# A power pooling on one core: three squares cut in two, with the root and the store of the load ahead between the parts

## The chip, the core and the metric

The kernel runs on one core of a Trainium2 chip. The metric is device time in microseconds (us), as the median of several executions. The core's engines that matter here are ScalarE (ACT), VectorE (DVE), SyncE (SP), which issues most transfers, and the 16 DMA engines that carry them. TensorE has no work, and GpSimd only writes four constants.

## The reference

Every window of four neighbours in a row is reduced to its power mean with p = 2, that is, the root of the mean of the squares:

```python
batch, channels, length = 32, 256, 4096
kernel_size = 4
...
window = np.abs(x[:, :, start:end]) ** p
result[:, :, i] = (np.mean(window, axis=-1)) ** (1.0 / p)
```

The input has 33.55 million float32 values (134.22 MB), the output a quarter of that (33.55 MB). Every output value depends on four adjacent input values alone, so the input can be cut anywhere at a multiple of four.

## The kernel before

The input is taken as one flat array and given to 128 partitions, 262,144 values each. It is worked through in 20 loads: 19 of 13,184 values per partition and a last one of 11,648. Three tiles of SBUF hold the loads in turn (load i goes to tile i mod 3), so load i + 3 can be issued only once the sums of load i have been read out of its tile.

Each load goes through four steps. ACT squares it in place (`square`, L88). DVE adds the values of a window two by two into the first half of the tile (`pairs`, L94), and adds those pairs into one value for each window (`fours`, L98). ACT takes the root with a scale of 1/4 (`root`, L101). The result is a quarter of a load, 3,296 values per partition.

The results of four loads make a block, and a block is stored with one transfer of the same size as a load (6,592 KB). Loads 0 to 3, 4 to 7, 8 to 11 and 12 to 15 are blocks; they all use one tile of results, `ot`, whose four quarters belong to the four loads. So the sums of the next block may overwrite a quarter only after the store of the block before has read it. To put this off, the sums of loads 4, 8, 12 and 16 go to a tile in PSUM (`st`), and their roots go from there to `ot` later. The sums of loads 5, 9 and 13 are the first that have to wait for the store. The results of loads 16 to 19 are kept in a tile of the loads that is free by then (`xt`), and are stored in two transfers.

The order of work on each engine is that of the program, written by hand (`manual_schedule`). SP issues all the loads (L82), each behind the sums of three loads earlier, and the last three stores. Stores 0, 1 and 2 are issued by ACT, on a DMA queue of its own (q10 in the profile; SP's is q1), right behind the root that completes them (L85). In a round of the main loop, ACT takes first the roots that stand in `ahead`, then the square of the load, then the roots that stand in `behind`:

```python
ahead = {4: (3,), 8: (7,), 12: (11,)}
behind = {3: [(0, 1, 2)], 7: [(5, 6), (4,)], 11: [(9, 10), (8,)], 14: [(12,)], 15: [(13, 14)], 16: [(15,)]}
```

So around load 4 ACT does: square of load 3, the roots of loads 0, 1 and 2 as one instruction, the root of load 3 as soon as DVE has its sum, the issue of store 0, and the square of load 4. Around loads 8 and 12 it is the same with the blocks after (there the roots of the block's first three loads are two instructions).

`implied(later, earlier)` tells the scheduler that no wait has to be made between two instructions, because other waits already put them in order. The last two loads, 18 and 19, have a part of their squares on DVE (L151), and their own order.

Of the kernel before, what the change touches and what calls it, by code (L numbers as in the profile page):

```python
# [1 line left out]

# [4 lines left out]


@with_exitstack
def kernel(  # L10
    ctx: ExitStack,
    tc: tile.TileContext,
    x: bass.AP,
    p: float,
    kernel_size: int,
    out: bass.AP,
):

    nc = tc.nc

    assert float(p) == 2.0, "kernel specialized for p == 2"
    k = int(kernel_size)  # L30
    assert k == 4, "kernel specialized for kernel_size == 4"

    P = nc.NUM_PARTITIONS
    fp32 = mybir.dt.float32
    Act = mybir.ActivationFunctionType
    add = mybir.AluOpType.add
    xf = x.rearrange("b c l -> (b c l)")
    of = out.rearrange("b c l -> (b c l)")
    total = xf.shape[0] // P

    W = 13184
    R = W // k
    X_SLOTS = 3
    LAST = total - 19 * W
    widths = [W] * 19 + [LAST]
    n = len(widths)
    assert 0 < LAST <= W and LAST % 16 == 0


    blocks = [[0, 1, 2, 3], [4, 5, 6, 7], [8, 9, 10, 11], [12, 13, 14, 15], [18, 16, 17], [19]]  # L50
    block_of = {i: b for b, group in enumerate(blocks) for i in group}
    block_width = [sum(widths[i] for i in group) for group in blocks]

    x_pool = ctx.enter_context(tc.tile_pool(name="x_pool", bufs=1))
    o_pool = ctx.enter_context(tc.tile_pool(name="o_pool", bufs=1))
    s_pool = ctx.enter_context(tc.tile_pool(name="s_pool", bufs=1, space=bass.MemoryType.PSUM))
    x_tiles = [x_pool.tile([P, W], fp32, name=f"xt{j}") for j in range(X_SLOTS)]
    o_tile = o_pool.tile([P, 4 * R], fp32, name="ot")
    first = o_pool.tile([P, 1], fp32, name="first")
    s_tile = s_pool.tile([P, 4096], fp32, name="st")  # L60
    ctx.enter_context(tc.manual_schedule())

    def rows(flat, b, div):
        at = sum(block_width[:b]) * P // div
        return flat[at:at + block_width[b] * P // div].rearrange("(p w) -> p w", p=P)


    free = x_tiles[17 % X_SLOTS]
    place = {i: o_tile[:, i % 4 * R:(i % 4 + 1) * R] for i in range(16)}
    place[18] = free[:, R:2 * R]  # L70
    place[19] = free[:, 0:LAST // k]
    place[16] = free[:, 2 * R:3 * R]
    place[17] = free[:, 3 * R:4 * R]
    held = [o_tile[:, :]] * 4 + [free[:, R:4 * R], place[19]]

    xs, loads, stores, sums = {}, {}, {}, {}

    def load(i):
        b = block_of[i]
        at = sum(widths[j] for j in blocks[b][:blocks[b].index(i)])  # L80
        xs[i] = x_tiles[i % X_SLOTS][:, 0:widths[i]]
        loads[i] = nc.sync.dma_start(out=xs[i], in_=rows(xf, b, 1)[:, at:at + widths[i]])  # L82

    def store(b, queue):
        stores[b] = queue.dma_start(out=rows(of, b, k), in_=held[b])  # L85

    def square(v):
        return nc.scalar.activation(out=v, in_=v, func=Act.Square)  # L88

    def pairs(v):  # L90

        q = v.rearrange("p (n j) -> p n j", j=k)
        h = v[:, 0:v.shape[1] // 2].rearrange("p (n j) -> p n j", j=2)
        return nc.vector.tensor_tensor(out=h, in0=q[:, :, 0:2], in1=q[:, :, 2:4], op=add)  # L94

    def fours(o, v):
        h = v[:, 0:v.shape[1] // 2].rearrange("p (n j) -> p n j", j=2)
        return nc.vector.tensor_tensor(out=o, in0=h[:, :, 0], in1=h[:, :, 1], op=add)  # L98

    def root(o, s):  # L100
        return nc.scalar.activation(out=o, in_=s, func=Act.Sqrt, scale=1.0 / k)  # L101

    summed = {i: s_tile[:, 0:R] if i in (4, 8, 12, 16) else place[i] for i in range(n)}

    def roots(*group):
        if len(group) == 1:
            root(place[group[0]], summed[group[0]])
        else:
            v = o_tile[:, group[0] % 4 * R:(group[-1] % 4 + 1) * R]
            r = root(v, v)  # L110
            if group[0] in (5, 9):

                implied(r, stores[block_of[group[0]] - 1])
        if group[-1] in (3, 7, 11):
            store(block_of[group[-1]], nc.scalar)

    def implied(later, earlier):

        tc.declare_no_dep(later.ins, earlier.ins, reason="implied by the other waits")

    for i in range(X_SLOTS):
        load(i)


    ahead = {4: (3,), 8: (7,), 12: (11,)}
    behind = {3: [(0, 1, 2)], 7: [(5, 6), (4,)], 11: [(9, 10), (8,)], 14: [(12,)], 15: [(13, 14)], 16: [(15,)]}

    root(first[:, :], nc.const_aps.tensor(1.0, (P, 1), fp32))
    for i in range(17):
        if i in ahead:  # L130
            roots(*ahead[i])
        s = square(xs[i])
        if i in (3, 7, 11):

            for earlier in sums[i - X_SLOTS]:
                implied(s, earlier)
        for group in behind.get(i, []):
            roots(*group)
        sums[i] = pairs(xs[i]), fours(summed[i], xs[i])
        if i + X_SLOTS < n:  # L140
            load(i + X_SLOTS)

    store(3, nc.sync)
    square(xs[17])
    pairs(xs[17])
    fours(summed[17], xs[17])
    later = {18: 4608, 19: 2000}

    def shared_square(i):
        v = xs[i][:, 0:later[i]]  # L150
        nc.vector.tensor_tensor(out=v, in0=v, in1=v, op=mybir.AluOpType.mult)  # L151
        square(xs[i][:, later[i]:widths[i]])

    def shared_pairs(i):
        implied(pairs(xs[i]), loads[i])

    shared_square(18)
    roots(16)
    roots(17)
    shared_pairs(18)  # L160
    fours(summed[18], xs[18])
    shared_square(19)
    roots(18)
    store(4, nc.sync)
    shared_pairs(19)
    fours(summed[19], xs[19])
    roots(19)
    store(5, nc.sync)


# [1 line left out]
_INS = ['x', 'p', 'kernel_size']  # L172
_OUTS = [((32, 256, 1024), 'float32')]

_NUMBERS = {'p': 2.0, 'kernel_size': 4}


# [26 lines left out]
```

## Time and profile before

| What | us |
|---|---|
| Median of 3 runs | 393.9 (393.82 to 394.01) |
| The profiled execution | 393.96 |
| Its span in the profile | 392.2 |
| ACT busy | 274.4 (70%), 37 instructions |
| DVE busy | 218.2 (56%), 42 instructions |
| ACT idle until a load landed | 90.9, 13 times |
| ACT idle until the sum of load 3, 7 or 11 was there | 7.0, 3 times |
| DVE idle until ACT had squared | 144.3, 18 times |
| DVE idle until a store had landed | 17.1, 3 times |
| A full load, issue to landing (median) | 29.7 |
| A store issued by ACT, issue to landing (median) | 35.1 |

Times inside the profile are counted from the start of its span. The profiled execution takes 1.8 us more than its span; what lies outside is not traced. In the lines of the timeline, the columns are the start, the duration, the engine, the line of the kernel, the operation with its tiles and shapes, how many such instructions were merged, and in brackets how long the engine was idle before and what ended that wait. In the groups by shape, the columns after the bar are the busy time in us, the mean of one instruction in ns, and the idle time just before them. "GB/s" in the slices and stretches counts a packet where it begins, so that short stretches are uneven.

### The profile page before, as it was taken

How to read it: one execution, taken by the hardware profiler on the slowest of the kernel's cores; microseconds unless marked ns; L12 is line 12 of the kernel's file. 1: busy time of each engine (PE TensorE's matmuls, PEld its weight loads, DVE VectorE, ACT ScalarE, POOL GpSimd, SP SyncE). 2: the span in 40 equal slices, each digit the busy share in tenths (PEclk: the TensorE clock that was granted, in tenths of full speed). 3: DMA queues.
4: the chain of work that ended last, by engine and by line, in shares of the span. 5: the costliest groups of instructions: out<-in, count | busy, mean ns of one | idle time of the engine just before them, and what ended most of it. 6: DMA issues, size and time to landing. Idle time of an engine off the chain costs nothing.

```text
span 392.2 us, 176 instructions
## 1 busy us (share of the span) xinstructions
DVE 218.2 (56%) x42; ACT 274.4 (70%) x37; POOL 0.2 (0%) x4
## 2 busy tenths in 40 slices
DVE  0008477490593374905942748069418485699980
ACT  1095685979950859799509597995098999969910
POOL 0000000000000000000000000000000000000000
DMA  8999999999999999999999999999999999999997
GB/s 344 430 430 441 436 436 441 436 436 387 430 430 430 430 430 430 430 436 430 446 441 452 446 441 436 430 430 430 430 430 430 430 430 430 430 428 438 430 413 342
DMA packets 3744, 167.77 MB, mean 428 GB/s; under 512 B 416, under 2 KB 416, under 8 KB 416
## 3 DMA queue, kind: packets, MB, share of 16 engines
q1 hardware_dynamic: 3312, 147.52, 87.4%
q10 hardware_dynamic: 432, 20.25, 11.9%
HBM read 134.22 MB, written 33.55 MB: 428 GB/s over the span
## 4 chain that ended last, share of the span: by engine, by line
DMA 43%; ACT 31%; DVE 23%; issue 0%; ACTq 0%; SPq 0%; DVEq 0%
DMA xt<-in_x_dram 43%; ACT xt L88 28%; DVE xt L94 14%; DVE ot L98 5%; DVE xt L98 3%; DVE xt L151 2%; ACT ot L101 2%; ACT xt L101 1%; ACTq L85 0%; SPq L82 0%; DVEq L94 0%
## 5 line engine op out<-in xcount | busy, mean ns | idle before, releaser
L88 ACT ACTIVATE xt<-xt 128x13184 f32<-128x13184 f32 (+2 forms) x20 | 216.7, 10847 | 92.2 <-DMA xt<-in_x_dram 90.9
L94 DVE TENSOR_TENSOR xt<-xt 128x6592 f32<-128x6592 f32 (+1 forms) x20 | 139.7, 6986 | 144.6 <-ACT xt L88 144.3
L98 DVE TENSOR_TENSOR ot<-xt 128x3296 f32<-128x3296 f32 x13 | 46.7, 3592 | 17.5 <-DMA out_dram<-ot 17.1
L101 ACT ACTIVATE ot<-ot 128x3296 f32<-128x3296 f32 (+2 forms) x8 | 37.2, 4656 | 7.0 <-DVE ot L98 7.0
L101 ACT ACTIVATE xt<-xt 128x3296 f32<-128x3296 f32 (+1 forms) x3 | 8.5, 2840 | 8.8 <-DVE xt L98 8.8
L98 DVE TENSOR_TENSOR st<-xt 128x3296 f32<-128x3296 f32 x4 | 14.4, 3600 | 0.1
L98 DVE TENSOR_TENSOR xt<-xt 128x3296 f32<-128x3296 f32 (+1 forms) x3 | 10.4, 3458 | 0.1
L101 ACT ACTIVATE ot<-st 128x3296 f32<-128x3296 f32 x3 | 8.7, 2899 | 0.0
L151 DVE TENSOR_TENSOR xt<-xt 128x4608 f32<-128x4608 f32 (+1 forms) x2 | 7.2, 3593 | 0.0
L101 ACT ACTIVATE xt<-st 128x3296 f32<-128x3296 f32 x1 | 2.9, 2899 | 0.0
L101 ACT ACT_TABLE_LOAD x1 | 1.3, 1283 | 0.7 <-PEq L185 0.7
L101 ACT ACTIVATE first<-const-float32-1.0 128x1 f32<-128x1 f32 x1 | 0.2, 203 | 0.0
L185 POOL MEMSET const-bfloat16-1.0<- 128x1 bf16 x1 | 0.1, 101 | 0.0
L185 POOL MEMSET const-uint8-127<- 128x1 uint8 x1 | 0.1, 101 | 0.0
L185 POOL MEMSET const-float32-0.0<- 128x1 f32 x1 | 0.1, 98 | 0.2 <-issue 0.2
L185 POOL MEMSET const-float32-1.0<- 128x1 f32 x1 | 0.1, 98 | 0.0
## 6 DMA issues: line engine op xcount, KB each, us to landing
xt<-in_x_dram SPq DMA_DIRECT2D x19, 6592.0 KB, 29.7
out_dram<-ot ACTq DMA_DIRECT2D x3, 6592.0 KB, 35.1
out_dram<-ot SPq DMA_DIRECT2D x1, 6592.0 KB, 37.0
xt<-in_x_dram SPq DMA_DIRECT2D x1, 5824.0 KB, 21.9
out_dram<-xt SPq DMA_DIRECT2D x1, 4944.0 KB, 16.1
out_dram<-xt SPq DMA_DIRECT2D x1, 1456.0 KB, 8.2
```

Of the source, the lines that this page charges most:

```text
L88: return nc.scalar.activation(out=v, in_=v, func=Act.Square)
L94: return nc.vector.tensor_tensor(out=h, in0=q[:, :, 0:2], in1=q[:, :, 2:4], op=add)
L98: return nc.vector.tensor_tensor(out=o, in0=h[:, :, 0], in1=h[:, :, 1], op=add)
L101: return nc.scalar.activation(out=o, in_=s, func=Act.Sqrt, scale=1.0 / k)
L151: nc.vector.tensor_tensor(out=v, in0=v, in1=v, op=mybir.AluOpType.mult)
L185: nc = _bacc.Bacc("TRN2", target_bir_lowering=False, num_devices=1)
```

## The change

The squares of loads 4, 8 and 12 are cut in two along the values: 7,600 and 5,584 for load 4, 7,296 and 5,888 for loads 8 and 12. The root of load 3, 7 or 11, and with it the issue of store 0, 1 or 2, moves from in front of the square to between its parts. DVE's sums of these loads still take the whole load, behind both parts. The other added lines are calls of `implied`, which leave out waits that the new parts would otherwise bring; the first part of such a square waits for its load, and the second part waits for nothing. No other instruction of any engine changes its place. The lines of the kernel behind the change move by up to 11.

```diff
-    ahead = {4: (3,), 8: (7,), 12: (11,)}
+    ahead = {4: 7600, 8: 7296, 12: 7296}
...
         if i in ahead:
-            roots(*ahead[i])
-        s = square(xs[i])
+            halves = square(xs[i][:, 0:ahead[i]]), roots(i - 1), square(xs[i][:, ahead[i]:W])
+        else:
+            s = square(xs[i])
         if i in (3, 7, 11):
 
             for earlier in sums[i - X_SLOTS]:
                 implied(s, earlier)
+        if i in (7, 11, 15):
+            implied(s, halves[0])
+            implied(s, halves[2])
         for group in behind.get(i, []):
             roots(*group)
         sums[i] = pairs(xs[i]), fours(summed[i], xs[i])
+        if i in ahead:
+            implied(sums[i][0], loads[i])
+            implied(sums[i][1], loads[i])
         if i + X_SLOTS < n:
             load(i + X_SLOTS)
+            if i in ahead:
+                implied(loads[i + X_SLOTS], loads[i])
...
-        square(xs[i][:, later[i]:widths[i]])
+        return square(xs[i][:, later[i]:widths[i]])
...
-    shared_square(18)
+    s = shared_square(18)
+    implied(s, halves[0])
+    implied(s, halves[2])
```

## The prediction

> **What bounds the kernel now.** I read three views, in this order. First the page's slices of the span, for the transfers:
>
> ```profile
> DMA  8999999999999999999999999999999999999997
> GB/s 344 430 430 441 436 436 441 436 436 387 430 430 430 430 430 430 430 436 430 446 441 452 446 441 436 430 430 430 430 430 430 430 430 430 430 428 438 430 413 342
> ...
> HBM read 134.22 MB, written 33.55 MB: 428 GB/s over the span
> ```
>
> The 16 DMA engines are busy in every slice, and the rate hardly moves, except for slice 10 (387, from 88.2 to 98.0 us), the two ends, and 413 near the end. Then the same by stretches (columns: stretch, its length, busy us of DVE, ACT and POOL, clock, DMA share, GB/s):
>
> ```profile
> 20.00:90.00 70.00, 42.47 (x8) 54.44 (x6) 0.00 (x0) 1.00 1.00 433
> 90.00:98.00 8.00, 0.00 (x0) 7.54 (x2) 0.00 (x0) 1.00 1.02 389
> 98.00:170.00 72.00, 42.48 (x8) 49.58 (x8) 0.00 (x0) 1.00 1.00 434
> ```
>
> DMA is at 1.00 throughout; ACT and DVE have idle time in each stretch. There is one weak place, 90 to 98 us. Third, the timeline, for the loads' landings, since a square that follows a wait for its load starts as that load lands:
>
> ```profile
> 65.95 11.19 ACT L88 ACTIVATE xt<-xt 128x13184 f32<-128x13184 f32 x1 [4.40 <-DMA xt<-in_x_dram]
> ...
> 87.86 2.95 ACT L101 ACTIVATE ot<-ot 128x3296 f32<-128x3296 f32 x1 [2.38 <-DVE ot L98]
> 90.84 0.38 ACTq L85 DMA_DIRECT2D out_dram<-ot  x1
> 91.27 22.27 ACT L88 ACTIVATE xt<-xt 128x13184 f32<-128x13184 f32 x2 [0.46 <-ACT ot L101]
> ...
> 144.40 11.19 ACT L88 ACTIVATE xt<-xt 128x13184 f32<-128x13184 f32 x1 [4.39 <-DMA xt<-in_x_dram]
> ...
> 222.26 11.19 ACT L88 ACTIVATE xt<-xt 128x13184 f32<-128x13184 f32 x1 [4.39 <-DMA xt<-in_x_dram]
> ...
> 300.10 11.19 ACT L88 ACTIVATE xt<-xt 128x13184 f32<-128x13184 f32 x1 [1.58 <-DMA xt<-in_x_dram]
> ```
>
> Those are the landings of loads 3, 7, 11 and 15. Between two of them lie five whole transfers, four loads and one store of the same size: 78.45, 77.86 and 77.84 us. Five times the 15.58 us between undisturbed landings (50.36 to 65.95) is 77.9. So the second and third blocks lose nothing to the compute engines, and the first loses 0.6 us, at the dip of 90 to 98 us.
>
> The sum of the whole span: 167.77 MB are 24.85 full transfers of 6.750 MB, at 15.57 us each 387.0. Ahead of them stand 3.6 us (load 0 lands at 19.20, less 15.57), the 0.6 us of the dip, and 0.9 us behind the last landing (the last store is issued at 383.16 and lands 8.2 us later, at 391.36): 392.1 of 392.2 us. The profiled execution took 393.96, 1.76 us outside the span; the median of the runs shown is 393.9.
>
> The chain of waits reads differently, and must not be taken at its word:
>
> ```profile
> DMA 43%; ACT 31%; DVE 23%; issue 0%; ACTq 0%; SPq 0%; DVEq 0%
> ```
>
> It follows a load back to its issue, and that to the sum and square that freed the slot. But the load's packets were queued behind other transfers then: load 7 is issued at 113.21 and lands at 144.40, 31.2 us for a transfer that takes 15.6 alone.
>
> **The change part by part.** *Two squares for one, three times.* From two rows by shape:
>
> ```profile
> L88 ACT ACTIVATE xt<-xt 128x9648 f32<-128x9648 f32 x1 | 8.2, 8243 | 0.8 <-DMA xt<-in_x_dram 0.8
> L88 ACT ACTIVATE xt<-xt 128x8576 f32<-128x8576 f32 x1 | 7.4, 7352 | 4.4 <-DMA xt<-in_x_dram 4.4
> ```
>
> 1072 elements more cost 891 ns: 0.831 ns each, and some 0.22 us are fixed. A part of 7600 takes 6.54 us, 5584 takes 4.86; 7296 takes 6.29, 5888 takes 5.12. Each split costs ACT 0.22 us.
>
> *ACT in block 1.* Now root (0, 1, 2) ends at 85.48, ACT waits 2.38 us for the sum of load 3, and root 3, store 0 and square 4 follow, ending at 102.46. Load 4 landed at 81.5 (issue 56.72 + 24.8), so the first part can start at 85.5 and ends at 92.0; the sum it would have waited for is ready at 87.83. Root 3 runs to 95.0, store 0 is issued from there (90.84 before: 4.2 us later), the second part ends at 100.3. Square 4 is 2.2 us earlier: 2.38 saved less 0.22. In blocks 2 and 3 the root of load 4 or 8 ends at 163.99 and 241.85, the waits are 2.33 us, and the same sum makes the stores 4.0 us later (173.25 and 251.1) and squares 8 and 12 2.1 us earlier.
>
> *What follows the earlier square.* DVE's two sums move with it, and load 7 is issued at 111.0, not 113.21. It is worth nothing: loads 5 and 6 and store 0 are still in the queues until 128 us, and load 7's packets stand behind load 6's. The same holds for loads 11 and 15. The cover is 15 us deep.
>
> *What follows the later store.* Its queue (ACT's) holds nothing else; behind its issue on ACT stands the second part, counted above. The one that waits for it is the sum of load 5 (9, 13) on DVE, which overwrites the stored tile; DVE waits 6.4, 5.5 and 5.3 us for the stores now. Store 0 lands 36.0 us after its issue, at 126.85. If that stays, it lands at 131.0. It could take longer, as its packets now begin after load 6's: before, the first came at 94.7, 3.8 us after the issue, with load 5 still running; now 98.8, when load 5 (undisturbed landing 81.5 + 15.6 = 97.1) is through and load 6 has had one packet of 1.95 us per engine (15.58 us for eight). At equal shares load 6 then finishes first and load 7 shares the rest, some 1.6 us more: 132.6. So the sum of load 5 ends at 134.6 to 136.2 and load 8 is issued at 134.7 to 136.3, against 130.61. It is late only if the queue has run dry: load 7 lands at 144.40, of which 0.7 is the tail of landing and 1.0 the way from issue to first packet (load 0: issue 0.73, first packets from 1.7). So it must be issued by 142.7: 6.4 us of cover are left of 12.1. For load 12 it is 212.1 to 213.8 against 220.6, for load 16 289.8 to 291.5 against 298.4. DVE's next work, the pairs of load 6, waits for a square that ends at about 138, after the late sum. Nothing is late next.
>
> *What the store meets.* The 0.6 us lost at 92 to 96 us is the one cost that the change could move. No row shows its cause. It stands at the first transfer of ACT's queue; at the second and third (issues at 169.29 and 247.15) the blocks lose nothing, and load 0, the first of SP's queue, also starts slowly (3.6 us ahead of 15.57, where later landings are 15.58 apart). That speaks for a price of a queue's first use, moved 4 us and paid again. From below it could vanish: -0.6, or -1.0 by the page's slice of 387 GB/s ((433 - 387) / 433 x 9.8 us). From above, it could double, +0.6. I take 0, as the nearest rows say first use.
>
> **A rule against it.** DVE waits for all three stores, and the trace of before shows 6.4 us of cover left behind a store 4 us later. The Trainium skill, DMA: Bandwidth & Descriptors, Rules for kernel authors, says to issue a transfer early and wait late, so that its fixed cost is covered. Read as a price, three stores 4 us later would add some 12 us (an estimate: the issue times above, by that rule) and give 406. Here the stores' lateness has its cover, and the sum goes by the rows.
>
> The sum: 0 from ACT, 0 from the stores, 0 from the dip: 392.2 us of span, 393.96 with what lies outside, 393.9 as a median.
>
> **The rivals.**
> - *The dip goes* (14%): the store starts at a boundary between loads and not amid load 5. For it: the dip lies where the store's first packets meet load 5's; against: blocks 2 and 3 had the same meeting and no dip. 393.3, at the least 392.9. Most of it (10%) is within 0.2%, 0.79 us, which is about what a measurement of this kernel can tell from no change.
> - *The chain is right* (3%): ACT's saved time shortens the path, 2.2 + 2.1 + 2.1 us: 387.5. Against it stand the DMA rows.
> - *Slower, the dip at each store* (7%): the store's first packets now meet a load's first packets three times. If the dip is the price of two transfers starting within about 2 us of each other, it comes in blocks 1, 2 and 3: 1.2 to 2.0 us more, 395.5. It decides as soon as blocks 2 and 3 lose 0.4 us each (0.8 together). Against: nothing in blocks 2 and 3 now.
> - *Slower, the queue runs dry* (3%): store 0 lands 6.4 us later than I allow and load 8 misses the end of load 7. At a third of the DMA instead of a half, the store would end with load 7, and sum, issue and first packet (2.4 us of landing, 3.6, 0.1, 1.0) would leave 7.1 us empty, three times: 415. Below that it costs nothing.
> - *It does not do what it says*: the order of instructions shows three more on ACT and none moved elsewhere, and load 4 is there in time. I give it nothing.
>
> **How the numbers follow.** No change 73%, between 393.5 and 394.5 with the dip's own bounds; the dip gone 14%; the others 13%. Faster by over 0.2%: 3 and 4 of the dip's 14, 7%. Slower: 7 and 3, 10%. Same: 83%. The range, 392.9 to 394.6, holds the first two cases, 87%.
>
> **What would show it.** Right: squares 7, 11 and 15 start at 144.4, 222.3 and 300.1 within 0.3 us; square 4's second part ends near 100.3; DVE waits 6 to 8 us longer for each store (its pairs come 2 us earlier, the store 4 to 6 later), 11 to 14 us each; DMA share stays 1.00; the dip of GB/s stands near 96 to 100 us. The dip gone: square 7 at 143.8. Wrong: a DMA share under 1.00 between 143 and 150, or a square 7 after 145.

## The result, and the profile after

The changed kernel takes 410.4 us (median of six runs, 405.5 to 412.6), the kernel before 394.0 (393.8 to 394.1). The ratio is 1.032, with a 95% interval of 1.028 to 1.037; it leaves out three of the six runs, which lie over 1.5% above the fastest one. Four more runs of it, beside other runs of the kernel before, gave 410.5 and 1.042 (1.040 to 1.043). Slower by 3 to 4%, then, where no change was forecast, and with 7 us between the first six runs where the kernel before has 0.3 (0.9 between the four later ones).

The page of the profiled execution (412.42 us, span 410.6) has these slices, DMA share in tenths and GB/s:

```profile
DMA  8999999999999999999999989999989899999695
GB/s 349 462 421 411 457 447 411 416 473 406 411 401 437 452 416 416 478 421 406 426 452 354 421 354 447 360 421 467 411 344 478 329 421 390 401 419 424 283 434 215
```

Before, the rate stood between 428 and 452 GB/s over nearly the whole span; now it falls to 354, 344, 329 and 283, and some slices have idle DMA engines. The stretches (start to end, length, busy us of DVE, ACT and POOL, clock, DMA share, GB/s) show where it begins:

```profile
20.00:90.00 70.00, 42.47 (x8) 56.80 (x6) 0.00 (x0) 1.00 1.00 433
90.00:98.00 8.00, 0.00 (x0) 7.55 (x3) 0.00 (x0) 1.00 1.10 461
98.00:135.00 37.00, 19.15 (x4) 14.71 (x3) 0.00 (x0) 1.00 0.98 410
135.00:170.00 35.00, 22.64 (x5) 30.61 (x5) 0.00 (x0) 1.00 1.00 434
```

Up to store 0 the two kernels are alike. While the store shares the DMA engines with load 6 (98 to 135 us) they are nearly as busy as before, 0.98 for 1.00, but move only 410 GB/s, where the kernel before moved 434 from 98 to 170 us. Alone again, the loads run at 434. The timeline has the landings:

```profile
65.77 11.19 ACT L88 ACTIVATE xt<-xt 128x13184 f32<-128x13184 f32 x1 [4.41 <-DMA xt<-in_x_dram]
...
94.59 0.38 ACTq L85 DMA_DIRECT2D out_dram<-ot  x1
...
133.24 11.19 ACT L88 ACTIVATE xt<-xt 128x13184 f32<-128x13184 f32 x1 [22.29 <-DMA xt<-in_x_dram]
133.50 3.59 DVE L98 TENSOR_TENSOR ot<-xt 128x3296 f32<-128x3296 f32 x1 [15.49 <-DMA out_dram<-ot]
...
148.82 11.19 ACT L88 ACTIVATE xt<-xt 128x13184 f32<-128x13184 f32 x1 [4.39 <-DMA xt<-in_x_dram]
...
232.99 11.19 ACT L88 ACTIVATE xt<-xt 128x13184 f32<-128x13184 f32 x1 [4.77 <-DMA xt<-in_x_dram]
...
316.37 11.19 ACT L88 ACTIVATE xt<-xt 128x13184 f32<-128x13184 f32 x1 [1.56 <-DMA xt<-in_x_dram]
```

Between the landings of loads 3, 7, 11 and 15 lie 83.05, 84.17 and 83.38 us, against 78.45, 77.86 and 77.84: 4.6, 6.3 and 5.5 us lost, 16.4 of the 18.4 by which the span grew. All three blocks lose, and about equally. The profile of the four later runs (span 408.5) has 82.77, 82.55 and 83.21 us between the same landings, so it shows the same. Load 6 lands at 133.24 (128.8 before), store 0 at 133.4.

### The profile page after: what moved, and what is told of

The parts are those of the page before. It is cut to its first block, busy times and chain, and to the rows that moved or that the text cites. A ratio compares the mean times of both kernels' runs of the same rounds, so it can differ in the third digit from the quotient of the medians.

```text
span 410.6 us, 179 instructions
## 1 busy us (share of the span) xinstructions
DVE 218.2 (53%) x42; ACT 274.3 (67%) x40; POOL 0.2 (0%) x4
## 4 chain that ended last, share of the span: by engine, by line
DMA 47%; ACT 33%; DVE 17%; issue 0%; ACTq 0%; SPq 0%; DVEq 0%
DMA xt<-in_x_dram 47%; ACT xt L88 27%; DVE xt L94 10%; ACT ot L101 5%; DVE ot L98 3%; DVE xt L98 3%; DVE xt L160 2%; ACT xt L101 1%; ACTq L85 0%; SPq L82 0%; DVEq L94 0%
## 5 line engine op out<-in xcount | busy, mean ns | idle before, releaser
L88 ACT ACTIVATE xt<-xt 128x13184 f32<-128x13184 f32 (+6 forms) x23 | 217.2, 9457 | 117.7 <-DMA xt<-in_x_dram 116.4
## 6 DMA issues: line engine op xcount, KB each, us to landing
out_dram<-xt SPq DMA_DIRECT2D x1, 4944.0 KB, 16.2
```

## The experiments

The first question was which part of the change does it: the cut square (three more instructions, loads 7, 11 and 15 issued 2 us earlier), or the store that comes 4 us later.

**A cut as short as ACT's wait.** The split alone, with the stores at their old places:

```diff
-    ahead = {4: 7600, 8: 7296, 12: 7296}
+    ahead = {4: 2600, 8: 2600, 12: 2600}
```

> The three squares stay cut in two, but the first parts are 2600 values long, 2.4 us, just as long as ACT waited in the kernel before. So the stores are issued when the kernel before issues them (90.8, 169.3, 247.2 us). If the later store is the cause, 394.0 within 0.3. If the cut itself is (more instructions, other waits, load 7 issued 2 us earlier), 405 or more.

394.1 (ratio 0.9998, 0.9984 to 1.0012), with store 0 issued at 90.7. The cut costs nothing, and gains nothing.

**The store later, nothing cut.**

```diff
 # against the kernel before
         if i in ahead:
+            for _ in range(8):
+                nc.scalar.activation(out=s_tile[:, R:4096], in_=place[i - 4][:, 0:4096 - R], func=Act.Square)
             roots(*ahead[i])
```

> Squares whole as in the kernel before, but ACT does eight small squares of results into unused PSUM (about 6.3 us, of no use to the result) ahead of the root of load 3, 7 or 11, so that the stores are issued about 4 us later than before, as in the changed kernel, and squares 4, 8 and 12 end 4 us later than before. If the later store is the cause: 403 to 412, like the changed kernel. If the cut is: 394 to 395.

396.3 (1.0056, 1.0033 to 1.0080), with store 0 issued at 95.1. Slower with no cut, but far from the changed kernel, and between the two forecasts: if the store is the cause, half a microsecond of difference in its issue matters more than the forecast allowed.

**The change for load 4 alone** (loads 8 and 12 keep root and store in front of the whole square).

> The change for load 4 alone; loads 8 and 12 as in the kernel before. If each late store costs for itself: a third of the loss, 398 to 400. If the DMA engines fall out of step once and stay so: nearly the whole, 404 or more. If the loss needs what adds up over three blocks: 394 to 395.

400.7 (1.0165, 1.0151 to 1.0179): some 40% of the loss. Its one late store costs 4.3 us before load 7 lands (82.77 us from load 3's landing to load 7's, against 78.45). The blocks whose stores are where they were lose another 1.0 and 0.5, so most of a late store's cost falls in its own block, and some behind it.

**The store later still, behind the whole square.**

```diff
 # against the kernel before
+        s = square(xs[i])
         if i in ahead:
             roots(*ahead[i])
-        s = square(xs[i])
```

> Squares whole, the root and the store behind them, so the stores are issued about 9 us later than in the kernel before, 5 later than in the changed one. If what counts is how late the store lands for the sums of load 5, 9 and 13, and so the next loads: slower than the changed kernel, 415 to 425. If what counts is that the store's first packets meet the first packets of a load: these meet load 6, 10 or 14 in its middle, and the time is 394 to 400.

394.2 (1.0000, 0.9986 to 1.0015). This run refuted lateness by itself as the cause. Its timeline:

```profile
99.33 0.38 ACTq L85 DMA_DIRECT2D out_dram<-ot  x1
...
134.51 3.59 DVE L98 TENSOR_TENSOR ot<-xt 128x3296 f32<-128x3296 f32 x1 [16.51 <-DMA out_dram<-ot]
```

The store is issued 8.5 us later than before and DVE waits until 134.5 for it, later than in the changed kernel, and it costs nothing. DVE's wait has the cover that the prediction gave it. So what counts is not how late the store is; where it meets the loads is the next candidate. Load 5's last packets end near 96 in the changed kernel.

**The store by SP, on the loads' queue** (the changed kernel with `store(block_of[group[-1]], nc.sync)`).

> The changed kernel with its cuts, but stores 0 to 2 are issued by SP, on the queue of the loads: each store stands whole between load 6 (10, 14) and the next, and no store shares the DMA engines with a load. If the loss comes from a load and a store sharing them, after a start near a load's end: 393.0 to 394.2; and if the 0.6 us dip of the kernel before was the first use of ACT's queue, it is gone too, 393.2 to 393.5. If the loss is in the cut squares or in the late store for DVE: 400 or more.

394.6 (1.0014, 1.0005 to 1.0023). Same cuts, same roots, but the store goes whole between load 6 and load 7, and the loss is gone but for half a microsecond (the forecast was 394.2 at the most). The dip is not gone: it stands in this run's twelfth slice (386 GB/s, 108 to 118 us), where the first store now begins.

```profile
GB/s 343 429 429 429 435 451 451 440 440 435 429 386 440 451 435 429 435 429 435 429 429 429 429 429 435 429 429 429 429 445 435 435 440 451 440 391 474 429 398 284
```

**Other lengths of the first part**: 5400, 9200 and 11,200 for load 4, each 304 less for loads 8 and 12.

> The changed kernel with first parts of 5400, 5096 and 5096 values, so that the stores are issued about 1.8 us earlier, 92.8 for the first (kernel before 90.8: 394; changed kernel 94.6: 405 and more). If a start of the store near the end of load 5 (about 96.5) is what costs, its packets begin at some 96 and it is as slow as the changed kernel, 400 or more. If the cost grows with the lateness of the store: 397 to 401.

> First parts of 9200, 8896 and 8896 values: stores issued about 1.3 us later than in the changed kernel, the first at 96.0, its packets from about 99.5, two packets behind the end of load 5. If only the meeting with the load's end costs: under 399. If it is the step between the DMA engines, which any start can upset: anything from 394 to 410, with several us between its runs.

> First parts of 11200, 10896 and 10896 values: stores issued about 3 us later than in the changed kernel, the first at 97.6, some 4 us behind the end of load 5 with its first packets. By the meeting with the load's end: 394 to 395, as with the store behind the whole square (99.3: 394.2). By lateness: over 405.

409.1 (1.0375, 1.0358 to 1.0393), 396.7 (1.0067, 1.0051 to 1.0084) and 394.05 (1.0003, 0.9994 to 1.0012).

**The middle of this row without a cut** (five of the small squares instead of eight), and **the load's end moved instead of the store**:

> Squares whole, five small squares into unused PSUM (4.3 us, no use to the result) ahead of the roots of loads 3, 7 and 11: the stores are issued at about 92.6 and 2 us later than before in the other blocks, as with first parts of 5400 (409), and squares 4, 8 and 12 end 2 us later than before. If the time of the store decides and the cut has no part in it: 403 to 411. If the cut or the earlier loads are needed for the loss: 394 to 397.

```diff
 # against the kernel before; the places in the results' tile follow
-    widths = [W] * 19 + [LAST]
+    widths = [W] * 5 + [LAST] + [W] * 14
```

> The kernel before, with no cut and no later store, but load 5 has 11,648 values per partition and load 19 has 13,184 (they change places in size), so load 5 ends 1.8 us earlier, near 94.4 instead of 96.2, while store 0 is still issued at 90.8: the same 3.6 us from issue to the load's end as with first parts of 5400. Blocks 2 and 3 are as before. If the distance from the store's issue to the load's end is the cause: 399 to 402, as with one late store. If it is the cut or the lateness: 394 to 395.

409.0 (1.0375, 1.0359 to 1.0390) and 403.8 (1.0215, 1.0154 to 1.0276). The second is the kernel before, its store at 90.7, and it loses about 10 us (5 in one of its four runs), more than the 5 to 8 forecast, as soon as load 5 ends 1.8 us earlier: 5.4 of them before load 7 lands (82.1 us from load 3's landing to load 7's, against 78.45 less the 1.8 that the shorter load saves), and 2 in each of the two blocks after, where the store comes no later. With the runs before, in the order of store 0's issue:

| Store 0 issued (us) | Kernel | Time (us) |
|---|---|---|
| 90.7 | first part 2600 | 394.1 |
| 90.8 | before | 394.0 |
| 92.6 | five fillers, no cut | 409.0 |
| 92.8 | first part 5400 | 409.1 |
| 94.6 | changed | 410.4 |
| 95.1 | eight fillers, no cut | 396.3 |
| 96.0 | first part 9200 | 396.7 |
| 97.5 | first part 11,200 | 394.05 |
| 99.3 | behind the square | 394.2 |

Between 90.8 and 97.5 us lies a window that is bad, whoever fills the time before it, and on both sides of it the time is that of before.

**Why the window.** The trace has a record of every DMA packet. A load and a store of full width are 128 packets each, one for each partition's row, eight on each of the 16 engines. Each packet begins where its engine's last one ended, so the records can be put back into 16 lanes (the numbering of the lanes is mine, and behind idle time the lanes are less sure, so I count block 1 alone). Two lanes of the changed kernel from 94 to 122 us; L is a load's packet, S a store's, with its us, and the first one listed is the last of load 5:

```
lane  1: L1.95 L1.95 L1.96 S2.01 L2.09 S1.95 L1.95 S1.95 L1.95 S1.95 L1.95 S1.95 L1.95 S1.95
lane 11: L1.95 L2.14 S1.95 L2.25 S2.44 L1.95 S2.66 L1.95 S2.72 L1.95 S2.66 L1.95 S2.41 L2.29
```

Once load and store alternate, a packet takes 1.95 us on nearly all lanes, but on three of them the store's mostly take 2.3 to 2.7. On those three the packets of 90 to 134 us take 4.1 to 5.4 us more in all than at 1.95 each, on the other 13 lanes 0.2 to 1.8. A load has landed when its last lane has, so three lanes hold up all, and 4.6 us is what the block lost. What sets lane 11 apart is the order: on lane 1 two packets of load 6 went ahead of the store, on lane 11 one. From then on they alternate, so on lane 11 the store's first row directly follows load 6's first row, its second the second, and so on. Over block 1 of 15 profiles (all but the store by SP and the half packets), by how many rows the load is ahead of the store's packet:

| Rows the load is ahead | Store packets | Mean us | Share over 2.05 us |
|---|---|---|---|
| -2 | 78 | 1.947 | 0% |
| -1 | 360 | 1.947 | 0% |
| 0 | 81 | 1.968 | 4% |
| 1 | 516 | 2.187 | 52% |
| 2 | 520 | 1.948 | 0% |
| 3 and 4 | 354 | 1.952 | 1% |

(At 0 the load's next packet is the one of the same row, and takes 2.1 to 2.3 us in the mean, by how the lanes are joined. In the table that moves the counts by up to a dozen, and the mean of 2.187 to 2.182. About half of the packets one row behind are not slow; what decides that stays open.) And by kernel: store packets one row behind the load number 0 in the kernel before and with 2600, 92 of 128 with 5400, 82 with five fillers, 75 with the narrow load, 29 and 37 in two profiles of the changed kernel, 44 in the change for load 4 alone, and 0 with 11,200 and behind the square; the 16 each with 9200 and eight fillers are the last packet of every lane, behind another store packet.

That is a reading of records, found after the fact: the order goes with the time. It makes two sharp forecasts: put one more packet ahead of the store on its queue, and the changed kernel (one or two rows behind the load) must recover, and the kernel before (level or ahead) must become slow.

```diff
 # against the changed kernel, first parts 430 shorter, and against the kernel before
+            b = block_of[group[-1]]
+            nc.scalar.dma_start(out=extra[:, b * 128:(b + 1) * 128], in_=o_tile[0:16, 3 * R:3 * R + 128])
             store(b, nc.scalar)
```

> The changed kernel with a small copy of 16 partitions (one packet for each DMA engine, from the results to an unused tile) on ACT's queue just ahead of each store; the first parts are 430 values shorter, so that the stores are still issued at 94.6 and at their places in blocks 2 and 3. The load gets ahead of the store by one more packet. If the slow packets are those where load and store are on the same partition's row: 394 to 397. If a start near the end of a load is what costs: 403 to 412.

> The kernel before, uncut, with the same small copy ahead of each store (the store's issue moves by 0.35 us, to 91.2). There the store is ahead of the load or level with it; one packet back brings engines to the same row. If the same row is the cause: 397 to 410. If the distance to the load's end is: 394 to 395.5, for 0.35 us is a fifth of the way to 92.8.

394.7 (1.0018, 1.0009 to 1.0027) and 410.3 (1.0405, 1.0389 to 1.0421). The issues of the copy and the store took a little longer than I had counted, so store 0 is issued at 94.9 in the first and 91.3 in the second; the second is 0.4 us from the kernel before and 16 us slower. In it, all the store's packets that could be placed in block 1 (125 of 128) are one row behind the load; in the first, none are. The copy also moves the store's issue by 0.3 to 0.4 us, but that shift alone is not what changed the order: with the store later still, at 92.8 (first part 5400), fewer packets, 92, are one row behind, and the load's lead of two to four rows in the first (54 packets at three, 70 at four) is more than the two to three rows with the store at 97.5. One stretch, 98 to 134 us, first of the recovered kernel, then of the spoilt one:

```profile
98.00:134.00 36.00, 17.65 (x3) 22.87 (x3) 0.00 (x0) 1.00 1.01 425
```

```profile
98.00:134.00 36.00, 17.65 (x3) 16.30 (x2) 0.00 (x0) 1.00 0.99 376
```

The DMA share is the same, 1.01 and 0.99; the packets take longer, and 376 GB/s are moved for 425.

**Half packets** (the changed kernel with every load and store in two transfers of half the width).

> The changed kernel, but every load and every store is issued as two transfers of half the width, so that the DMA engines alternate between load and store in packets of 26 KB instead of 52.7. If engines that fall out of step by part of a packet are the cause, half the packet is half the loss or less: 394 to 401. If the start of the store at the load's end costs whatever the packets are: 405 to 412.

396.3 (1.0053, 1.0038 to 1.0068). It agrees, but settles nothing: with twice as many packets the number of rows by which a load is ahead is another, too.

**The changed kernel again, beside those runs.**

> The changed kernel once more, on the same chip as these runs, for its profile beside theirs: 405 to 413, with more spread between its runs than the kernel before has.

410.5. On three of its lanes in block 1 the store is one row behind the load from the first packet on, and 37 store packets are so in all.

**An early small write**, to settle the dip:

> The kernel before with one small store more, of one value per partition, at 2 us, into the place that store 0 overwrites later. If the dip of 0.6 us at 92 to 96 us is the price of the program's first write to the output, it moves to the start, beside the slow first packets of load 0: 393.4 to 393.7. If it is the price of a store beside a load, 394.0 to 394.3.

394.2 (1.0005, 0.9996 to 1.0014): not moved. The rate in the ten microseconds from 88 to 98 is 406 GB/s with it and without it.

## Why the prediction was wrong, point by point

- **The DMA engines bound the kernel**: right before, and in the main after, where they are idle for 3.3% of the span. So is the warning on the chain of waits: ACT's two microseconds per block were worth nothing (the cut of 2600 has them and takes 394.1).
- **ACT's times**: right. The first part took 6.52 us (6.54 worked out), root 3 and the store followed at 94.59 (95.0), square 4 ended at 99.9 (100.3), load 7 was issued at 110.6 (111.0).
- **The later store is covered for DVE**: right as a cover, and shown by the store behind the square, which DVE gets at 134.5 without loss. The landing was put at 131.0 to 132.6 and came at 133.4 in the changed kernel; DVE waited 15.5 to 16.2 us for each store, not 11 to 14. The prediction's own sign of being wrong, a square 7 after 145, came: 148.82.
- **The step that failed** is the one headed "What the store meets", and the sum's "0 from the stores". It looked for a price only in the 0.6 us dip, and took each packet of a load and a store at 1.95 us, in whatever order they alternate. I had even worked out that load 6 would have "one packet of 1.95 us per engine" of a start, which is the order that the lanes show to be slow: a store's packet there took 2.2 us in the mean and mostly 2.3 to 2.7 on the slow lanes, and the blocks lost 4.6, 6.3 and 5.5 us instead of nothing.
- **The dip as a queue's first use**: wrong. It stands at the first store also when SP's queue carries it, after seven loads on that queue. That a small write ahead of it changes nothing leaves its cause open.
- **The rival "the dip at each store"** had the right place, the store's first packets at a load's first packets, and the right condition, a loss in all three blocks. Its mechanism and price (1.2 to 2.0 us) were not right: the loss is no start-up price but goes on while the two alternate.
- **The rival "the queue runs dry"** plays a part, at another price and for another reason than the one it gave, a store at a third of the DMA. The DMA queues of the changed kernel (packets, MB, share of 16 engines over the span):

```profile
q1 hardware_dynamic: 3312, 147.52, 85.1%
q10 hardware_dynamic: 432, 20.25, 11.6%
```

  96.7% of 410.6 us are 397.1 us of packets on the mean engine; before, 87.4 and 11.9% of 392.2 were 389.4. So of the 18.4 us by which the span grew, the mean engine spent 7.7 in longer packets and 10.7 idle. Its idle time follows from the slow lanes: a load can be issued only when the sums of the load three earlier are done, and the sum of load 5, 9 or 13 waits for a store, so for the store's slowest lane. By then the lanes have come up to 12 us apart, and the fast ones run out of packets. Load 16 waits for this sum of load 13:

```profile
301.06 3.59 DVE L98 TENSOR_TENSOR ot<-xt 128x3296 f32<-128x3296 f32 x1 [15.82 <-DMA out_dram<-ot]
```

  It is issued at 304.72. Eight of the 16 lanes are out of packets at that moment; the last lane is through with load 15 at 316:

```profile
300.00:304.00 4.00, 2.94 (x1) 3.18 (x1) 0.00 (x0) 1.00 1.00 435
304.70:305.70 1.00, 0.00 (x0) 1.00 (x1) 0.00 (x0) 1.00 0.51 158
306.00:316.00 10.00, 3.96 (x1) 8.81 (x2) 0.00 (x0) 1.00 0.84 364
```

  The share falls from 1.00 to 0.51. How much time such gaps add of themselves, beyond the wait for whichever lane is slow, stays open.
- **A rule against it.** The Trainium skill, DMA: Bandwidth & Descriptors, Rules for kernel authors, says to issue a transfer early and to wait for it late, so that its fixed cost overlaps with other work. I set it aside with reason: a store 8.5 us later cost nothing here. That the estimate of 406 made from it lies near the measured time is chance. The same page, Queues, rings and completion order, says that an engine goes round the queues packet by packet; the lanes show it, one row of each in turn.

Not settled is what the two packets share, the SBUF partition or something on the memory's side that goes with the row. That each engine takes the rows of a load and of a store in the same order is inferred, not traced. Nor does the order of the rows explain the 2 to 3 us that are lost with eight fillers and with 9200, where load packets on one or two lanes go slow two rows ahead.

No version beat the kernel before. Cuts of 2600 and 11,200 have its time.

## What to carry to other kernels

Where two transfers of the same shape share the DMA engines, compare not only shares and bytes, but the order in which their packets alternate: a busy share near 1.00 with fewer GB/s is the sign here, and the price is that the 16 engines finish one transfer at different times. Before you judge a transfer "later" or "earlier", move it over several microseconds in both directions; one point can stand in a window that its neighbours miss. And where a kernel with no slack is at its best, ask which order of transfers it owes that to: here 0.4 us and one small packet lost it.

## What the runs showed that I had not expected

- A store's packet that follows the load's packet of the same place in its transfer on the same DMA engine: 2.187 us in the mean, over 2.05 in 52% of 516; with the load one row further ahead, 1.948 and 0% of 520.
- One more packet per engine (8 KB in all) ahead of a store turned 394.0 into 410.3, and the changed kernel's 410.4 into 394.7.
- The slow kernels can scatter: the changed one by 7 us in six runs, though by 0.9 in four others. Those with the time of before stay within 1.2.
- The first block with a store loses some 0.5 to 0.6 us more than the next two, with the store on ACT's queue as on SP's.
